# Hybrid layer on one core: the state-space layer's rotation tables for two groups and its other weights for four at once, on VectorE instead of GpSimd, and the states' product one group later

## The chip, the core and the metric

The kernel runs on one core of a Trainium2 chip. The time is that of one execution on the device, in microseconds (us). Five engines work side by side, each on a list of instructions in a fixed order: TensorE (PE, and PEld for its weight loads), VectorE (DVE), ScalarE (ACT), GpSimd (POOL), and SyncE (SP), which here only issues DMAs between DRAM and the core's memory, SBUF. PSUM is the memory that TensorE writes its products to. Times come from the hardware profiler's trace of one execution.

## What is computed

One decoder layer, depth 1, 2048 tokens of 1024 dimensions. After an RMS norm, one projection gives u, z_s, q, k, v and z_a of 512 columns each. u goes through a state-space layer, q, k and v through differential attention; both are gated, concatenated and projected back, and a second gated input is added. The change is in the state-space layer alone:

```python
ab_re = mag * jnp.cos(li * dt)
ab_im = mag * jnp.sin(li * dt)
...
bu_re = jnp.einsum('bsgp,gnp->bsgn', ug, bb_re)
bu_im = jnp.einsum('bsgp,gnp->bsgn', ug, bb_im)
...
_, _, xr, xi = lax.associative_scan(combine, (a_re, a_im, bu_re, bu_im), axis=1)
y = (jnp.einsum('bsgn,gpn->bsgp', xr, c_re.astype(f32))
     - jnp.einsum('bsgn,gpn->bsgp', xi, c_im.astype(f32)))
y = y.reshape(bsz, s_len, SSM_WIDTH) + d_skip.astype(f32) * uf
y = jax.nn.gelu(y)
y = y * jax.nn.sigmoid(y @ glu_w.astype(f32) + glu_b.astype(f32))
```

There are 32 groups (g) of 16 channels (p); each drives 64 complex states (n).

## The kernel before

**Phases.** Phase 1 (0 to some 745 us) makes the projections in 12 blocks of 512 columns, in the order u, u, then k, zs, v, q, za for the first half of the tokens and zs, k, v, q, za for the second. Every float32 factor is split into a pair of a rounded part (h) and a rest (l), and a product is three matmuls. The weights of a block come as eight tiles (`wraw`, line 275), are split by ScalarE (`wh`, 278) and VectorE (`wl`, 279), and lie in a ring of eight pairs, so that the next block's loads start as the last matmuls of this block let the ring go. Phase 2 is the attention, phase 3 the output.

**The state-space layer** runs in the background of phase 1: the generator `ssm` (309) is advanced a few steps after each quarter of a block. A scheduler that works from an estimate of durations and from priorities then fixes the order of each engine's list; background work has the lower priority.

**A group.** The tokens are cut into 256 chunks of 8 steps; a group's inputs U are 128 rows (8 steps by 16 channels) by 256 chunks. For each group the loop of line 563 does this:

- loads U (572), multiplies it with the norm's factors on GpSimd (573) and splits it (518, 519);
- makes the group's table of rotations `tab`, cosines and sines of 272 chunk phases: four products on GpSimd (584 to 587) and a difference and a sum on VectorE (588, 589);
- makes the weights out of the state, `wc`: three instructions on GpSimd (597 to 599) and a split;
- splits its part of the weights within a chunk, `mg`;
- multiplies `wa` with U into the first half of a PSUM bank (617), turns the result with the table (`rotate`, 604: three instructions `md`, `sw`, `md` on VectorE, two half copies `sw` on ScalarE), scans it over the chunks (`zz`, 621), turns it back and splits it (`xa`, 623);
- multiplies `mg` with U and then `wc` with `xa` into the second half of the bank (624, 625), and writes the result out (627, 628).

For each four groups, `four` (526) loads the parameters, makes `na` on GpSimd (534 to 538) and from it, on TensorE, `M` (through DRAM, 550 and 554) and `wa`. When all groups are done the GLU follows (line 676), for 256 tokens at a time.

Of the kernel before, what the change touches and what calls it, by code (L numbers as in the profile page):

```python
# [11 lines left out]
F32 = mybir.dt.float32  # L12
# [3 lines left out]
ALU = mybir.AluOpType  # L16
# [3 lines left out]
D = 1024  # L20
# [4 lines left out]
L = 8  # L25
# [34 lines left out]
TTB = 1  # L60
# [5 lines left out]
FA = 1  # L66
# [6 lines left out]
SSE = (1, 0, 0)  # L73
# [7 lines left out]
SPB = dict(U=2,wa=2,wc=2,mg=2,xa=1)  # L81
SPE = (1, 1, 1, 1)
# [5 lines left out]
SWB = 2  # L88
# [5 lines left out]
class Streamer:  # L94
    """Runs the making of a sequence of ring tiles ahead of their use."""
# [23 lines left out]
def hymba_kernel(ctx, tc, x_t, p_t, positions, norm_w, w_in, lam_re, lam_im, log_dt, b_re, b_im,  # L119
# [4 lines left out]
    TE, NE, UE = ((G, V)[v_] for v_ in SSE)  # L124
# [7 lines left out]
    NPAR = 9 * 2 + 16 * 4 + 16 * 2 + 17 * 2 + 1 + 9 * 2  # L132
    par_scr = [tc.dram_tile([128, 4, NPAR], F32, name=f"par_scr{i}") for i in range(8)]
    zs_scr = tc.dram_tile([512, S], F32, name="zs_scr")
# [19 lines left out]
    def reduce_angle(pool, src, shape, tag):  # L154
        """src - 2 pi round(src / 2 pi), and its cosine's angle; both within [-pi, pi]."""
# [8 lines left out]
        # a quotient next to a half may have been rounded away from its side  # L164
# [9 lines left out]
    def exp_exact(pool, out_, src, shape, tag):  # L174
        """exp to float32's accuracy: 2^k times a polynomial of the rest."""
# [17 lines left out]
    # ------------------------------------------------------------------ phase 1  # L193
    with ExitStack() as p1:
# [3 lines left out]
        # a place for each unit in the ring; what is used last lies lowest  # L198
# [13 lines left out]
        # -- x, split: units of 256 tokens, the model's dimensions on the partitions  # L212
# [32 lines left out]
        def squares(unit):  # L245
            """The mean squares of a unit's tokens, down the partitions."""
# [45 lines left out]
        # the first two units and the first weights, in the order of use  # L292
# [15 lines left out]
        # -- state-space layer, in the background of the projections  # L308
        def ssm():
            # tables of rotary embedding and small constants  # L310
            with tc.tile_pool(name="p1s", bufs=1) as sp:
# [16 lines left out]
                # lambda  # L328
# [12 lines left out]
                for nm, src in (("q", q_norm_w), ("k", k_norm_w)):  # L341
                    # the norm's weights: in the rotation's tables, and for what isn't turned down the partitions
# [846 lines left out]
```

## Time and profile before

| | us |
|---|---|
| median of three runs | 1517.39 |
| lowest and highest run | 1514.34, 1518.22 |
| span of the profiled execution (first to last instruction) | 1513.9 |
| TensorE busy in the span | 1423.3 (94%) |
| VectorE busy | 1015.2 (67%) |
| ScalarE busy | 755.2 (50%) |
| GpSimd busy | 648.0 (43%) |

The profiled execution's own time isn't listed apart from the three runs; its span is the part of it that the trace shows. "Busy" is the time in which an engine has an instruction running; matmuls are pipelined, one starting before the last has ended, so a busy TensorE isn't one at its peak. The shares are averages over phases with different limits; the rows further below are of the stage in which the change lies.

### The profile page before, as it was taken

Reading aid. Unit: us, or ns where it says so; the run is one execution under the profiler, and the core shown is the slowest. Engines: PE = TensorE matmul, PEld = TensorE weight load, DVE = VectorE, ACT = ScalarE, POOL = GpSimd, SP = SyncE. Lnnn points to the kernel's source line nnn. Section 1 sums busy time; section 2 is a strip of 40 time slices with the busy share of each in tenths; the row PEclk is TensorE's granted clock in tenths of the full one; section 3 lists DMA queues with packets and bytes.
Section 4 is the critical chain, followed back from the end, with each engine's and each line's share of the span. In section 5 each row is a group of like instructions: output and inputs, shape, how many; then the busy total and the mean of one; then the engine's idle time right before and its main releaser. Section 6 shows DMA issues by size and latency. Waiting matters only on the chain.

```text
span 1513.9 us, 27895 instructions
## 1 busy us (share of the span) xinstructions
PE 1423.3 (94%) x9794; PEld 1308.5 (86%) x9794; DVE 1015.2 (67%) x2489; ACT 755.2 (50%) x1711; POOL 648.0 (43%) x902
## 2 busy tenths in 40 slices
PE   7899988997988999999899999899999999999998
PEld 7898887776777888888789888898999999999998
DVE  8579899998999786665377767667779543222222
ACT  8443344544664455533358677677878541111111
POOL 5632666787757341132134445445434442221110
PEclk9999999999999999999999999999999999999999
DMA  7437824334553377634973543544426442111101
GB/s 237 137 114 249 278 82 138 126 88 143 178 155 103 118 187 201 167 119 152 241 213 97 153 137 108 156 122 122 136 80 208 126 152 91 64 63 64 63 22 43
DMA packets 208245, 205.56 MB, mean 136 GB/s; under 512 B 61016, under 2 KB 163560, under 8 KB 207080
## 3 DMA queue, kind: packets, MB, share of 16 engines
q1 hardware_dynamic: 208104, 203.78, 45.0%
q8 instruction: 77, 1.26, 0.3%
q14 instruction: 64, 0.52, 0.1%
HBM read 137.56 MB, written 74.55 MB: 140 GB/s over the span
## 4 chain that ended last, share of the span: by engine, by line
PE 52%; DVE 20%; DMA 12%; POOL 6%; issue 5%; ACT 3%; SPq 2%; DVEq 0%; ACTq 0%; POOLq 0%
PE pm L1125 11%; PE pss L1007 7%; PE pmf L892 7%; PE po L1043 7%; PE pmm L793 6%; PE pm L892 4%; PE ptw L1039 3%; PE pm L1129 3%; DMA wraw<-in_w_in_dram 3%; PE pss L676 2%; PE pmm L747 2%; DVE sw L611 2%; DVE md L612 1%; DVE wl L279 1%; DVE zz L621 1%
## 5 line engine op out<-in xcount | busy, mean ns | idle before, releaser
L793 PE MATMUL pmm<-wl,xh 128*128 128x512 f32 x512 | 202.9, 398 | 2.6 <-DVE wl L279 2.6
L793 PE MATMUL pmm<-wh,xh 128*128 128x512 f32 x512 | 200.2, 397 | 4.5 <-ACT wh L278 4.5
L793 PE MATMUL pmm<-wh,xl 128*128 128x512 f32 x512 | 202.4, 397 | 0.0
L1007 PE MATMUL pss<-ks,qd 128*128 128x512 f32 (+3 forms) x640 | 185.3, 388 | 5.5 <-DMA qd<-qh_scr 3.3
L1018 ACT ACTIVATE s<-s,st 128x1024 f32<-128x1024 f32 (+4 forms) x192 | 171.5, 896 | 35.7 <-DVE st L1009 32.6
L1043 PE MATMUL po<-vt,wt 128*128 128x128 f32 x1088 | 149.6, 276 | 2.3 <-ACT yo L1055 1.3
L1043 PEld LDWEIGHTS po<-vt,wt 128*128 128x128 f32 x1088 | 139.8, 191 | 10.0 <-ACT yo L1055 2.9
L1009 DVE CUSTOM_DVE_ANT_0 s<-pss,mk,st 128x512 f32<-128x512 f32 (+2 forms) x192 | 122.1, 650 | 39.3 <-PE pss L1007 37.9
L1125 PE MATMUL pm<-xh,wgh 128*128 128x256 f32 x512 | 141.3, 282 | 1.9 <-ACT xh L1095 1.8
L1125 PE MATMUL pm<-xh,wgl 128*128 128x256 f32 x512 | 142.8, 281 | 0.0
L1125 PE MATMUL pm<-xl,wgh 128*128 128x256 f32 x512 | 142.4, 281 | 0.0
L747 PE MATMUL pmm<-xh,wh 128*128 128x256 f32 x448 | 125.1, 293 | 8.9 <-DVE stg L757 4.0
L747 PE MATMUL pmm<-xh,wl 128*128 128x256 f32 x448 | 127.7, 289 | 0.7 <-DVE wl L279 0.7
L1133 DVE SCALAR_TENSOR_TENSOR th<-th,pm 128x256 f32<-128x256 f32 x64 | 26.7, 420 | 150.7 <-ACT th L1132 150.7
L747 PE MATMUL pmm<-xl,wh 128*128 128x256 f32 x448 | 127.1, 287 | 0.0
L1096 POOL TENSOR_TENSOR xl<-x,xh 128x512 fp32r<-128x512 f32 x32 | 43.2, 1366 | 179.7 <-PE pm L1125 110.7
L793 PEld LDWEIGHTS pmm<-wh,xh 128*128 128x128 f32 x512 | 97.9, 191 | 23.7 <-ACT wh L278 4.9
L793 PEld LDWEIGHTS pmm<-wl,xh 128*128 128x128 f32 x512 | 97.7, 191 | 23.3 <-DVE wl L279 5.0
L892 PE MATMUL pmf<-yh,woh 128*128 128x256 f32 x352 | 104.2, 296 | 11.5 <-ACT yh L882 9.0
L1007 PEld LDWEIGHTS pss<-ks,qd 128*128 128x128 f32 x640 | 101.3, 192 | 14.7 <-DVE st L1009 4.9
L793 PEld LDWEIGHTS pmm<-wh,xl 128*128 128x128 f32 x512 | 97.9, 191 | 18.3
L1132 ACT ACTIVATE th<-pm 128x256 f32<-128x256 f32 x64 | 24.3, 385 | 166.9 <-PE pm L1129 165.3
(360 smaller groups left out, 4294.5 us busy)
## 6 DMA issues: line engine op xcount, KB each, us to landing
wraw<-in_w_in_dram SPq DMA_DIRECT2D x96, 256.0 KB
xraw<-in_x_t_dram SPq DMA_DIRECT2D x40, 256.0 KB
qd<-qh_scr SPq DMA_DIRECT2D x64, 128.0 KB
qd<-ql_scr SPq DMA_DIRECT2D x64, 128.0 KB
xr<-in_x_t_dram SPq DMA_DIRECT2D x32, 256.0 KB
yin<-yt_scr SPq DMA_DIRECT2D x16, 512.0 KB
xp_scr<-xp SPq DMA_DIRECT2D x32, 256.0 KB
x<-xp_scr SPq DMA_DIRECT2D x8, 1024.0 KB
```

The source lines that it names most:

```text
L611: V.tensor_tensor(sw, sw, tabf[:, 1, first:first + NCH], op=ALU.mult)
L747: T.matmul(pm, lhsT=w[b_][:, cb * 128:cb * 128 + 128], rhs=xt[a_][:, k, :], start=(k == 0 and n == 0), stop=(k == 7 and n == 2))
L793: T.matmul(pm, lhsT=xt[a_][:, k, j * 128:j * 128 + 128], rhs=w[b_], start=(k == 0 and n == 0), stop=(k == 7 and n == 2))
L892: T.matmul(pm[:, e, :], lhsT=w[k][b_][:, ms], rhs=y[a_][:, k, :], start=(k == 0 and n == 0), stop=(k == 3 and n == 2))
L1007: T.matmul(pss[:, :cl], lhsT=qd[:, e, m, tq], rhs=ks[m][:, c0:c0 + cl], start=e == 0, stop=e == 1)
L1009: V.tensor_tensor_reduce(sr[m][pi][:, o:o + cl], pss[:, :cl], mk[:, end - cl:end], scale=1.0, scalar=3.4e38 if ci == 0 else st[:, 2 * ci - ...
L1018: A.activation(sr[m][pi][:, :cl], sr[m][pi][:, :cl], AF.Exp, bias=st[:, ci + m:ci + m + 1], scale=-1.0, accum_out=st[:, 12 + 2 * pi + m:13 ...
L1039: T.transpose(ptw[:, k, :], blocks_[kg + k], ident)
L1043: T.matmul(po[:, 0:128], lhsT=wt[:, k, :], rhs=vt[:, kg + k, :], start=kg + k == 0, stop=kg + k == len(blocks_) - 1)
L1096: G.tensor_tensor(xl, x1[:, n0:n0 + 2], xh.bitcast(F32), op=ALU.subtract)
L1125: T.matmul(pm[:, 0], lhsT=wg[0][k][b_][:, ms], rhs=xc[k // 2][a_][:, k % 2], start=(k == 0 and n == 0), stop=(k == 7 and n == 2))
L1129: T.matmul(pm[:, 1], lhsT=wp[0][k][b_][:, ms], rhs=pc_[a_][:, k], start=(k == 0 and n == 0), stop=(k == 1 and n == 2))
```

## The change

The setup makes the phase tables for half as many columns, with two groups over the 128 partitions (64 states each), and writes them to a DRAM array of their own (`ptab_scr`). `four` becomes a generator in four parts, advanced once a group: parameters and `na`; M and `wa`; the tables of the two pairs of groups; `wc` of all four groups. All of it but the mask of `dd` is on VectorE. A pair's table is written to DRAM (`tab_scr`) and read back in two halves for each group, so that both halves of the partitions hold it; the sign that was in the table is now in ScalarE's copy (`A.mul` with -1). The splits of `mg` and `wc` are made for four groups at once. U and the table of the next group are fetched one group ahead (`ahead`). All six products of U are issued together, and the product of the states is issued after the next group's (`behind`).

```diff
-SSE = (1, 0, 0)
+SSE = 0
...
-SPB = dict(U=2,wa=2,wc=2,mg=2,xa=1)
-SPE = (1, 1, 1, 1)
+SPB = dict(U=2, wa=2, wc=1, mg=1, xa=1)
...
-SWB = 2
+SWB = 1
...
-    TE, NE, UE = ((G, V)[v_] for v_ in SSE)
+    UE = (G, V)[SSE]
...
+                tp = sp.tile([128, NG // 2, NTAB], F32, name="tp")
...
+                def spread(par4, o_, l0):
+
+                    r_ = sp.tile(sh, F32, name="na", bufs=1)
+                    t_ = sp.tile([128, 2, 17, 16], F32, name="tabt", bufs=1).rearrange("q s a b -> q (s a b)")[:, :512]
+                    t_ = t_.rearrange("q (g l p) -> q g l p", g=4, l=L)
+                    V.tensor_tensor(r_, par4[:, :, o_:o_ + 16].unsqueeze(2).to_broadcast(sh),
+                                    par4[:, :, 65 + l0:73 + l0].unsqueeze(3).to_broadcast(sh), op=ALU.mult)
+                    V.tensor_tensor(t_, par4[:, :, o_ + 16:o_ + 32].unsqueeze(2).to_broadcast(sh),
+                                    par4[:, :, 74 + l0:82 + l0].unsqueeze(3).to_broadcast(sh), op=ALU.mult)
+                    V.tensor_tensor(r_, r_, t_, op=ALU.add)
+                    return r_
...
-                    G.tensor_tensor(na, par4[:, :, 18:34].unsqueeze(2).to_broadcast(sh),
-                                    par4[:, :, 150:158].unsqueeze(3).to_broadcast(sh), op=ALU.mult)
-                    G.tensor_tensor(nb, par4[:, :, 34:50].unsqueeze(2).to_broadcast(sh),
-                                    par4[:, :, 159:167].unsqueeze(3).to_broadcast(sh), op=ALU.mult)
-                    NE.tensor_tensor(na, na, nb, op=ALU.add)
...
+                    pt2 = sp.tile([128, 2, NTAB], F32, name="pt2", bufs=1)
+                    nc.sync.dma_start(pt2, ptab_scr[q4])
+                    na = spread(par4, 0, 1)
...
+                    for e in range(2):
+                        tx = sp.tile(sht, F32, name="tx", bufs=1)
+                        t1 = sp.tile(sht, F32, name="tabt", bufs=1)
+                        V.tensor_tensor(tx, pt2[:, e, 0:17].unsqueeze(1).unsqueeze(3).to_broadcast(sht),
+                                        pt2[:, e, 34:66].rearrange("q (s b) -> q s b", s=2).unsqueeze(2).to_broadcast(sht), op=ALU.mult)
+                        V.tensor_tensor(t1, pt2[:, e, 17:34].unsqueeze(1).unsqueeze(3).to_broadcast(sht),
+                                        pt2[:, e, 66:98].rearrange("q (s b) -> q s b", s=2).unsqueeze(2).to_broadcast(sht), op=ALU.mult)
+                        V.tensor_tensor(tx, tx, t1, op=ALU.add)
+                        nc.sync.dma_start(tab_scr[q4 * 2 + e], tx)
+                    yield
+                    wc = spread(par4, 32, 0)
+                    out_[q4] = par4, wa, M, wc
+                    yield
...
+                def ahead(g):
+
+                    U = sp.tile([128, NCH], F32, name="U", bufs=UB)
+                    nc.sync.dma_start(U, ug_scr[g].rearrange("l p c -> (l p) c"))
+                    UE.tensor_tensor(U, U, rl, op=ALU.mult)
+                    tab = sp.tile([128, 2, 17, 16], F32, name="tab")
+                    for d in range(2):
+                        nc.sync.dma_start(tab[d * 64:d * 64 + 64], tab_scr[g // 2][(g % 2) * 64:(g % 2) * 64 + 64])
+                    return split(U, "U", NCH), tab.rearrange("q s a b -> q s (a b)")
...
-                    G.tensor_tensor(tab[:, 0], ab[0], bb[0], op=ALU.mult)
-                    G.tensor_tensor(t1[:, 0], ab[1], bb[1], op=ALU.mult)
-                    G.tensor_tensor(tab[:, 1], ab[0], bb[1], op=ALU.mult)
-                    G.tensor_tensor(t1[:, 1], ab[1], bb[0], op=ALU.mult)
-                    TE.tensor_tensor(tab[:, 0], tab[:, 0], t1[:, 0], op=ALU.subtract)
-                    TE.tensor_tensor(tab[:, 1], tab[:, 1], t1[:, 1], op=ALU.add)
...
-                    wc = split(wc, "wc", 128, SPE[1])
...
-                    mg = split(M[:, :, gl * 16:gl * 16 + 16], "mg", 128, SPE[2])
...
+                    product(pst, [w_[:, gs] for w_ in wa4], U)
+                    product(py, [w_[:, gs] for w_ in mg4], U, last=False)
+                    if behind is not None:
+                        behind()
+                    if gl == 0:
+                        wc4 = split(wc_raw.rearrange("q g l p -> q (g l p)"), "wc", 512)
...
-                    product(pst, wa, U)
...
-                    product(py, mg, U, last=False)
-                    product(py, wc, xa, first=False)
...
+                    next(parts, None)
+                    if gl == 3 and g < NG - 1:
+                        mg4 = within(made[g // 4 + 1][2])
+                    if g < NG - 1:
+                        nxt = ahead(g + 1)
                     yield
+                behind()
```

What the scheduler makes of it is seen in the engines' lists. On TensorE, in the q block of the first half, before (`pss` is the bank of a group and `pmm` one of the projections; the number behind a name tells its instances apart):

```order
L524 MATMUL pss_3813<-Uh_3792,wah_3371 128x256
L524 MATMUL pss_3461<-xal_3487,wch_3457 128x256
L524 MATMUL pss_3461<-xah_3486,wcl_3458 128x256
L793 MATMUL pmm_4276<-wl_3608,xh_789 128x512
L524 MATMUL pss_3813<-Ul_3793,wah_3371 128x256
L524 MATMUL pss_3813<-Uh_3792,wal_3372 128x256
L524 MATMUL pss_3695<-Uh_3674,mgh_3696 128x256
L524 MATMUL pss_3695<-Ul_3675,mgh_3696 128x256
L524 MATMUL pss_3695<-Uh_3674,mgl_3697 128x256
```

and now, in the same block:

```order
L526 MATMUL pss_3612<-Uh_3436,wah_2784 128x256
L526 MATMUL pss_3612<-Ul_3437,wah_2784 128x256
L526 MATMUL pss_3612<-Uh_3436,wal_2785 128x256
L526 MATMUL pss_3612<-Uh_3436,mgh_3129 128x256
L526 MATMUL pss_3612<-Ul_3437,mgh_3129 128x256
L526 MATMUL pss_3612<-Uh_3436,mgl_3130 128x256
```

Before, a group's products with `wa` and with `mg` stood apart, with another group's between them (the `mg` products of 3813 begin 36 rows behind its first `wa` product); now the six products of one U stand in a row, and the products with `wc` follow apart from them.

On GpSimd, within the layer, before:

```order
L573 TENSOR_TENSOR U<-U,rl 128x256
L585 TENSOR_TENSOR tabt<-parg 128x272
L587 TENSOR_TENSOR tabt<-parg 128x272
L584 TENSOR_TENSOR tab<-parg 128x272
L586 TENSOR_TENSOR tab<-parg 128x272
L597 TENSOR_TENSOR wc<-parg 128x128
```

and now (`dd` is the skip's diagonal, `qst` the norm of queries and keys):

```order
L553 AFFINE_SELECT dd<-dd 128x64
L592 TENSOR_TENSOR U<-U,rl 128x256 x5
L553 AFFINE_SELECT dd<-dd 128x64
L592 TENSOR_TENSOR U<-U,rl 128x256 x2
L841 TENSOR_SCALAR qst<-qst 128x8
L842 TENSOR_TENSOR qst<-qst,negh 128x8
```

Of a group's eight instructions one, U's, has stayed there.

On SP, where the loads of the weights (`wraw`) follow the za block of the first half, before (`za_scr` takes that block's result, `yg_scr` a group's):

```order
L275 DMA wraw<-in_w_in_dram 128x512
L808 DMA za_scr<-t_5774 128x512
L628 DMA yg_scr<-ysb 128x256
L275 DMA wraw<-in_w_in_dram 128x512
L572 DMA U<-ug_scr 128x256
L275 DMA wraw<-in_w_in_dram 128x512 x3
```

and now, at the end of the same loads:

```order
L275 DMA wraw<-in_w_in_dram 128x512
L591 DMA U<-ug_scr 128x256
L275 DMA wraw<-in_w_in_dram 128x512
L595 DMA tab<-tab_scr_96 64x544 x2
L275 DMA wraw<-in_w_in_dram 128x512
L582 DMA tab_scr_97<-tx 128x544
```

The table's reads and the next table's write have come between the loads of the weights.

## Rows read from the trace of the kernel before

**Rows 1.** One stretch: busy us per engine (instructions), clock, DMA share, GB/s.

```profile
190.00:500.00 310.00, 271.84 (x1556) 233.26 (x1554) 292.20 (x576) 156.49 (x380) 219.84 (x287) 0.96 0.41 125
```

**Rows 2.** VectorE's groups, 190 to 500 us: busy us, mean ns, idle us.

```profile
L612 DVE TENSOR_TENSOR md<-md,sw 128x256 f32<-128x256 f32 x60 | 37.1, 618 | 0.5
L611 DVE TENSOR_TENSOR sw<-sw,tab 128x256 f32<-128x256 f32 x60 | 34.0, 568 | 4.2 <-ACT sw L610 3.6
L279 DVE SCALAR_TENSOR_TENSOR wl<-wraw,nw,wh 128x512 fp32r<-128x512 f32 x32 | 27.4, 864 | 5.6 <-ACT wh L278 5.6
L621 DVE TENSOR_TENSOR_SCAN zz<-parg,md 128x256 f32<-128x256 f32 x30 | 25.4, 848 | 0.3
L519 DVE TENSOR_TENSOR Ul<-U,Uh 128x256 fp32r<-128x256 f32 x31 | 21.3, 687 | 0.0
L519 DVE TENSOR_TENSOR xal<-md,xah 128x256 fp32r<-128x256 f32 x29 | 19.2, 663 | 0.0
L588 DVE TENSOR_TENSOR tab<-tab,tabt 128x272 f32<-128x272 f32 x30 | 18.9, 630 | 2.2 <-POOL tab L584 1.7 <-POOL tabt L585 0.5
L608 DVE TENSOR_TENSOR md<-zz,tab 128x256 f32<-128x256 f32 x30 | 16.8, 559 | 0.5
L519 DVE TENSOR_TENSOR mgl<-M,mgh 128x128 fp32r<-128x128 f32 x32 | 16.0, 500 | 0.0
L589 DVE TENSOR_TENSOR tab<-tab,tabt 128x272 f32<-128x272 f32 x30 | 15.9, 529 | 0.0
L519 DVE TENSOR_TENSOR wcl<-wc,wch 128x128 fp32r<-128x128 f32 x29 | 13.3, 460 | 1.9 <-ACT wch L518 1.8
```

**Rows 3.** VectorE, whole span: shortest, median, longest ns by line.

```profile
L612 DVE TENSOR_TENSOR md<-md,sw x64: 408/456/1296, 192.7 to 515.2; 128x256 f32<-128x256 f32 x64
...
L608 DVE TENSOR_TENSOR md<-pss,tab x32: 405/412/426, 189.2 to 506.0; 128x256 f32<-128x256 f32 x32
...
L621 DVE TENSOR_TENSOR_SCAN zz<-parg,md x32: 675/694/1771, 194.4 to 512.2; 128x256 f32<-128x256 f32 x32
...
L279 DVE SCALAR_TENSOR_TENSOR wl<-wraw,nw,wh x96: 721/750/1775, 5.4 to 702.5; 128x512 fp32r<-128x512 f32 x96
...
L519 DVE TENSOR_TENSOR wal<-pss,wah x8: 675/678/679, 187.4 to 460.7; 128x512 fp32r<-128x512 f32 x8
```

**Rows 4.** TensorE's waits, 190 to 500 us: total us, times, longest us.

```profile
PE pss L524 <- DVE xal L519: 11.3, 14, 1.9
PE pmm L793 <- ACT wh L278: 4.5, 1, 4.5
PE pss L524 <- ACT sw L610: 3.2, 5, 1.1
```

**Rows 5.** GpSimd's groups, 190 to 500 us, of the kinds that stay.

```profile
L573 POOL TENSOR_TENSOR U<-U,rl 128x256 f32<-128x256 f32 x31 | 29.4, 949 | 26.3 <-DVE zz L620 12.3 <-DMA U<-ug_scr 5.9 <-DVE t L772 2.8
...
L815 POOL TENSOR_TENSOR qst<-qst,negh 128x8 f32<-128x8 f32 x8 | 14.4, 1797 | 0.4
...
L546 POOL TENSOR_SCALAR_AFFINE_SELECT dd<-dd 128x64 f32<-128x64 f32 x6 | 2.7, 444 | 10.2 <-DMA dd<-in_ssm_d_dram 10.2
```

**Rows 6.** Timeline at 336 us: start us, duration us, engine.

```profile
335.84 1.72 POOL L815 TENSOR_TENSOR qst<-qst,negh 128x8 f32<-128x8 f32 x1
...
336.10 0.41 DVE L519 TENSOR_TENSOR Ul<-U,Uh 128x256 fp32r<-128x256 f32 x1
```

**Rows 7.** Two stretches of projections alone: as rows 1.

```profile
50.00:60.00 10.00, 10.00 (x86) 10.00 (x85) 6.88 (x22) 3.61 (x7) 5.98 (x10) 1.00 0.45 117
680.00:690.00 10.00, 10.00 (x48) 8.29 (x47) 4.92 (x13) 1.27 (x2) 4.37 (x6) 1.00 0.32 105
```

**Rows 8.** Timeline of the first group: U's multiplication and the first product.

```profile
178.97 0.74 POOL L573 TENSOR_TENSOR U<-U,rl 128x256 f32<-128x256 f32 x1
...
187.46 0.28 PE L524 MATMUL pss<-Uh,wah 128*128 128x256 f32 x1
```

**Rows 9.** ScalarE's waits, 190 to 500 us: total us, times, longest us.

```profile
ACT wh L278 <- DMA wraw<-in_w_in_dram: 16.8, 11, 7.3
```

More of the change, by code (lines that the diff above doesn't have):

```diff
@@ L59 @@
 XRB = 3
-TTB = 1
 GLE = (0, 2)
@@ L65 @@
 BGS = (1, 0)
-FA = 1
 KOUT = (0, 3)
@@ L536, in four @@
-                    G.tensor_tensor(nb, par4[:, :, 34:50].unsqueeze(2).to_broadcast(sh),
-                                    par4[:, :, 159:167].unsqueeze(3).to_broadcast(sh), op=ALU.mult)
-                    NE.tensor_tensor(na, na, nb, op=ALU.add)
-                    pr_ = ps_ss.tile([128, 512], F32, name="pss")
-                    for g in range(4):
-                        T.matmul(pr_[:, g * 16:g * 16 + 16], lhsT=na[:, g].rearrange("q l p -> q (l p)"),
-                                 rhs=par4[:, g, 50:66], start=True, stop=True)
+                    pt2 = sp.tile([128, 2, NTAB], F32, name="pt2", bufs=1)
@@ L547, in four @@
                                     fill=0.0, base=-112, channel_multiplier=1)
+                    yield
+                    pr_ = ps_ss.tile([128, 512], F32, name="pss")
+                    for g in range(4):
+                        T.matmul(pr_[:, g * 16:g * 16 + 16], lhsT=na[:, g].rearrange("q l p -> q (l p)"),
+                                 rhs=par4[:, g, 32:48], start=True, stop=True)
                     rs = sp.tile([128, 64], F32, name="rs", bufs=1)
@@ L557, in four, with within @@
                         T.transpose(pw_[:, g * 128:g * 128 + 128], na[:, g].rearrange("q l p -> q (l p)"), ident)
-                    wa = split(pw_, "wa", 512, 1)
-                    return par4, wa, M
-                nxt = four(0)
+                    wa = split(pw_, "wa", 512)
+                    yield
+                    sht = [128, 2, 17, 16]
+                    for e in range(2):
[7 more added lines that the diff above has]
+                        nc.sync.dma_start(tab_scr[q4 * 2 + e], tx)
+                    yield
+                    wc = spread(par4, 32, 0)
+                    out_[q4] = par4, wa, M, wc
+                    yield
+                def ahead(g):
[3 more added lines that the diff above has]
+                    tab = sp.tile([128, 2, 17, 16], F32, name="tab")
+                    for d in range(2):
+                        nc.sync.dma_start(tab[d * 64:d * 64 + 64], tab_scr[g // 2][(g % 2) * 64:(g % 2) * 64 + 64])
+                    return split(U, "U", NCH), tab.rearrange("q s a b -> q s (a b)")
+                def within(M):
+                    return split(M.rearrange("q l (g p) -> q g l p", g=4), "mg", 512)
+                made = {}
+                for _ in four(0, made):
+                    pass
+                mg4 = within(made[0][2])
+                nxt = ahead(0)
+                behind = None
                 yield
@@ L564, in ssm @@
                     gl = g % 4
+                    gs = slice(gl * 128, gl * 128 + 128)
                     if gl == 0:
[L566 to L572 removed]
@@ L598, in ssm @@
-                    G.tensor_tensor(nb, q1b, K2.unsqueeze(1).to_broadcast(shl), op=ALU.mult)
-                    NE.tensor_tensor(wc, wc, nb, op=ALU.add)
-                    wc = split(wc, "wc", 128, SPE[1])
-                    bank = ps_ss.tile([128, 512], F32, name="pss")
-                    mg = split(M[:, :, gl * 16:gl * 16 + 16], "mg", 128, SPE[2])
+                        par4, wa4, _, wc_raw = made.pop(g // 4)
+                        parts = four(g // 4 + 1, made) if g < NG - 4 else iter(())
```

110 lines of the change are left out of this document (44 added, 66 removed).

## The prediction

> **What bounds the kernel now.** I read the table of stretches first, since the average over the span hides the stage that is changed. From 190 to 500 us, while 30 of the 32 groups of the state-space layer run behind the projections, VectorE is busy 292.2 of 310 us (94%) and TensorE 271.8 [rows 1]. So TensorE has 38 us idle there, and its granted clock is 0.96 on average, which is 12 us more of lost work. It isn't the bound. VectorE is.
>
> Next, what VectorE does there, line by line [rows 2]. The 256-element instructions of one rotation (md, sw) cost 618, 568 and 559 ns on average, and the same shapes have run in 408 ns; the same multiplication with its source in PSUM (md<-pss) never took more than 426 ns in all 32 runs [rows 3]. So a third of what these lines cost is waiting of some kind, and it strikes instructions whose two inputs both lie in SBUF. GpSimd is busy 219.8 us of the same 310 [rows 1], nearly all with two-input work on SBUF.
>
> Last, who TensorE waits for [rows 4]: xal 11.3 us and sw 3.2 us, both the states' rotation on VectorE and ScalarE, and once 4.5 us for weights.
>
> **The change part by part.** The sum is made for the stage from 190 to 500 us of the profiled execution, whose span is 1513.9 us; the median of the three runs, 1517.4, lies 3.5 us above that span, and the sum's difference is put to the median.
>
> *Removed from VectorE.* The two closing instructions of each group's table (18.9 + 15.9 us), and the splits of the within-chunk weights (mgl, 16.0) and of the weights out of the state (wcl, 13.3): 64.1 us [rows 2].
>
> *Added to VectorE.* Per two groups, three instructions of 544 elements for the table; per four groups, six of 512 (the two spreads) and two splits of 512. A 512-element two-input instruction has 678 ns (wal, [rows 3]) and a 256-element one 408, so 1.05 ns an element, and 544 elements come to 0.71 us. For 30 groups that is 15 x 3 x 0.71 = 32.0 and 7.5 x 8 x 0.678 = 40.7, together 72.7 us. wal has one source in PSUM and the new ones broadcast both sources from SBUF; no row shows that on VectorE. If they paid what md<-md,sw pays over its floor (618 against 408 ns, [rows 2, 3]), they would cost half as much again, 109 us. Below 72.7 they can't go, since that is the price of the same element count undisturbed. I take 72.7: the disturbing instructions are the ones that leave. Net +8.6 us, at worst +45.
>
> *Relief.* What stays on VectorE (md, sw, zz, Ul, xal and the weights' wl) costs more than its floor by 60 x 0.210 + 60 x 0.160 + 30 x 0.173 + 31 x 0.279 + 29 x 0.255 + 30 x 0.151 + 32 x 0.143 = 52 us [rows 2, 3], with 408 ns as the floor of all 256-element ones. On GpSimd five kinds stay, from U (29.4 us) to dd (2.7), with three qst lines between: 54.3 us [rows 5]. So 165.5 of 219.8 us leave. But the long qst instruction doesn't disturb: while one ran from 335.84 for 1.72 us, Ul took its 0.41 us [rows 6]. Counting U alone as what goes on disturbing, 165.5 / (165.5 + 29.4) = 85% of the 52 us goes, 44 us. Bounds: 0, if the excess is something else, and 52.
>
> The Trainium skill (SBUF — State Buffer, section "Who interferes with whom") says that a VectorE instruction with two SBUF inputs contends with a GpSimd instruction that reads SBUF, and that the loser blocks for the whole instruction. By the forms that are slow here and the PSUM form that isn't, the trace agrees; in the row at 335.84 us it doesn't, since a GpSimd instruction that reads SBUF ran and nothing was held. By the rule qst would keep on disturbing, 75% would go instead of 85%, 39 us, and the time below would be some 5 us longer.
>
> *Sum on VectorE.* 292.2 + 8.6 - 44 = 256.8 us. If VectorE is then busy as large a part of the stage as now, 256.8 / 0.943 = 272 us instead of 310: -38, and for 32 groups instead of 30, -40.
>
> *The states' product one group later.* Now a group's product within the chunk waits until both halves of the rotation have read the bank, and its last product follows a few matmuls behind xal. In the new order all six products of U stand together, and xal has a group's time. That takes away the 11.3 and 3.2 us of waits [rows 4]. It is no second gain: these waits are where TensorE feels VectorE's lateness, and they lie within the 38 us.
>
> *The start.* The first product stands 92 matmuls of the zs block earlier than before; a 10 us stretch holds 86 of them [rows 7], so 10.7 us earlier. Before, it ran at 187.46 us [rows 8]. Its operands come no 10 us earlier: U was multiplied at 178.97 for 0.74 us [rows 8], with a cast and Ul (0.41 each) behind it, so 180.6 us at the earliest, while TensorE is there at 176.8. I charge the difference, 4 us, with 0 and 10.7 as the bounds (M now has to be back from DRAM at once too).
>
> *DMAs.* Tables go out once per two groups and come back in two halves per group: 16 + 64 more transfers on SP's queue, 8 + 8 for their parameters. The transfers are covered by the group's time that they have; what stands behind them in the queue is the first rival of the other sign, below. The table of half as many groups in the setup shortens VectorE's work ahead of 160 us, where TensorE doesn't wait for it: 0.
>
> *The end.* The last product of the layer stands 137 matmuls later, and the GLU behind it too. After GLU's last matmul 306 of the 512-element matmuls of the projections still follow before and 169 in the new order; at 48 matmuls in 10 us [rows 7] that is 35 us of cover left: 0.
>
> Total: -40 + 4 = -36 us, 1517.4 - 36 = 1481.
>
> **The rivals.** *TensorE becomes the bound.* If the relief is complete and the decoupling takes the rest, all 38 us idle and the 12 us of clock go: 1517 - 50 + 4 = 1471, and less if the short gaps that pipelined matmuls hide in "busy" go too. For it: at full relief VectorE would need 249 us for work in which TensorE is busy 272 [rows 1]. Against it: weights and DMA make waits of their own (4.5 us for wh).
>
> *The relief doesn't come.* The excess may be the price of broadcast and small tiles rather than of GpSimd. Then VectorE has 300 us or more to do, and only the waits on xal and sw go: -14.5, with 4 to 10.7 us lost at the start: 1507 to 1514. For it: the new instructions have forms that no row prices. Against it: md<-pss with its steady 412 ns.
>
> *SP's queue takes VectorE's place: slower.* The table's write waits for VectorE, its reads wait for the buffer that the rotation two groups back still reads, and in the new order they stand among the loads of the next block's weights. At a block's change eight such loads are due at once; ScalarE already waits 16.8 us for them, 7.3 at the longest [rows 9], and TensorE's single 4.5 us is that wait. The stage has six such changes. From 36 / 6 = 6 us each the gain is gone; at 8.5 us each the kernel is at 1532. Against it: SP already waits for Ul with U's load in just that place, and these waits shrink with VectorE's work.
>
> That the change doesn't do what it says is excluded by the order of GpSimd's instructions, where tables and weights are gone.
>
> **How the numbers follow.** Forecast 0.45 (1476 to 1490), TensorE as the bound 0.22, no relief 0.20, SP's queue 0.13. The predicted time is the forecast's, 1481. About 0.3% (4.6 us) is what a measurement of this kernel can tell from no change, so "same" is 1512.8 to 1522: of the no-relief case 0.06 falls there, and 0.02 of the SP case. Faster: 0.45 + 0.22 + 0.14 = 0.81; same 0.08; slower 0.11. For 8 in 10 the range needs the forecast, the TensorE case with its hidden gaps and most of the no-relief case: 1456 to 1513.
>
> **What would show it.** In the new profile, over the stretch of the layer: md, sw and xal near 410 ns; the table's instructions at 0.71 us; VectorE's busy time down by some 35 us; TensorE's waits on xal and sw gone; the first product of the layer behind a wait of some 4 us. I am wrong if md<-zz stays above 500 ns with GpSimd idle, if the 544-element instructions cost 1 us, or if ScalarE's wait for wraw grows to tens of us.

## The result, and the profile after

Four runs of the changed kernel took 1476.78 to 1481.17 us, median 1479.18; four of the kernel before 1512.88 to 1518.22, median 1515.87. The ratio is 0.9754, with a 95% interval of 0.9732 to 0.9776: 36.7 us less. The prediction was 1481, from 1456 to 1513. The profiled execution took 1478.0 us with a span of 1476.3.

Where the time went is seen when the span is cut at the last 512-element matmul of the projections, the end of phase 1. That matmul starts at 740.9 us in the kernel before and at 704.6 now; from there to the end it is 773.0 us before and 771.7 now. So 36.3 of the 37.6 us are gone ahead of that point.

The stretch from 190 to 500 us, columns as in [rows 1]:

```profile
190.00:500.00 310.00, 299.94 (x1791) 261.87 (x1791) 273.83 (x609) 167.10 (x361) 62.11 (x70) 0.99 0.58 177
```

TensorE is busy 28.1 us longer in the same 310 us and does 235 more matmuls; its idle time is 10.1 us instead of 38.2. GpSimd is down from 219.8 to 62.1 us. VectorE is down from 292.2 to 273.8, although it does the work of 31 groups instead of 30 and of more projections. The layer itself isn't shorter: its first product starts at 187.5 us and its last at 519.4 before, at 175.0 and 511.4 now. The projections get on faster beside it.

VectorE's groups by line in this stretch (line, operation, out<-in, count, busy us, mean ns, idle before):

```profile
L279 DVE SCALAR_TENSOR_TENSOR wl<-wraw,nw,wh 128x512 fp32r<-128x512 f32 x40 | 29.9, 751 | 6.6 <-ACT wh L278 6.5
L633 DVE TENSOR_TENSOR md<-md,sw 128x256 f32<-128x256 f32 x61 | 27.3, 448 | 0.7
L632 DVE TENSOR_TENSOR sw<-sw,tab 128x256 f32<-128x256 f32 x62 | 27.1, 437 | 4.8 <-ACT sw L631 4.5
L640 DVE TENSOR_TENSOR_SCAN zz<-parg,md 128x256 f32<-128x256 f32 x31 | 21.8, 703 | 0.4
L521 DVE TENSOR_TENSOR xal<-md,xah 128x256 fp32r<-128x256 f32 x30 | 13.6, 455 | 1.6 <-ACT xah L520 1.4
L629 DVE TENSOR_TENSOR md<-zz,tab 128x256 f32<-128x256 f32 x31 | 13.3, 430 | 0.4
L629 DVE TENSOR_TENSOR md<-pss,tab 128x256 f32<-128x256 f32 x31 | 12.9, 415 | 0.0
L521 DVE TENSOR_TENSOR Ul<-U,Uh 128x256 fp32r<-128x256 f32 x30 | 12.5, 415 | 3.2 <-ACT Uh L520 3.2
L537 DVE TENSOR_TENSOR tabt<-parg 128x512 f32<-128x512 f32 x15 | 11.0, 731 | 0.8 <-DMA parg<-par_scr 0.7
L539 DVE TENSOR_TENSOR na<-na,tabt 128x512 f32<-128x512 f32 x15 | 10.7, 715 | 0.0
L577 DVE TENSOR_TENSOR tx<-pt 128x544 f32<-128x544 f32 x14 | 10.6, 756 | 13.4 <-DMA tab_scr<-tx 13.4
L579 DVE TENSOR_TENSOR tabt<-pt 128x544 f32<-128x544 f32 x14 | 10.0, 712 | 0.0
L581 DVE TENSOR_TENSOR tx<-tx,tabt 128x544 f32<-128x544 f32 x14 | 9.9, 711 | 0.0
L535 DVE TENSOR_TENSOR na<-parg 128x512 f32<-128x512 f32 x14 | 9.5, 680 | 0.0
...
L521 DVE TENSOR_TENSOR wcl<-na,wch 128x512 fp32r<-128x512 f32 x8 | 6.4, 806 | 0.2 <-ACT wch L520 0.2
...
L521 DVE TENSOR_TENSOR mgl<-M,mgh 128x512 fp32r<-128x512 f32 x7 | 4.8, 686 | 0.0
```

md, sw, xal and Ul come from 559 to 687 ns [rows 2] down to 415 to 455; md<-pss, with one input in PSUM, stays at 415 as it was at 412. TensorE's waits in the stretch (total us, times, longest us):

```profile
PE pmm L820 <- ACT wh L278: 2.3, 2, 1.3
...
PE pss L526 <- DVE xal L521: 0.5, 1, 0.5
```

The 11.3 us on xal and the 3.2 on sw [rows 4] have become 0.5 and nothing.

### The profile page after: what moved, and what is told of

The parts are those of the page before. It is cut to its first block, busy times and chain, and to the rows that moved or that the text cites. A ratio compares the mean times of both kernels' runs of the same rounds, so it can differ in the third digit from the quotient of the medians.

```text
span 1476.3 us, 27658 instructions
## 1 busy us (share of the span) xinstructions
PE 1409.7 (95%) x9794; PEld 1299.4 (88%) x9794; DVE 971.7 (66%) x2477; ACT 749.0 (51%) x1663; POOL 468.8 (32%) x654
## 4 chain that ended last, share of the span: by engine, by line
PE 40%; DMA 7%; ACT 2%; DVE 2%; POOL 1%; issue 1%; SPq 1%; DVEq 0%; ACTq 0%; POOLq 0%
PE pm L1152 11%; PE po L1070 6%; PE pss L1034 6%; PE pmf L919 6%; PE pm L919 4%; PE pm L1156 3%; PE ptw L1066 3%; DMA yin<-yt_scr 2%; DMA ks<-kh_scr 1%; DMA yin<-in_ple_w_gate_dram 1%; DMA qd<-ql_scr 1%; DMA yt_scr<-yo 1%; ACT s L1045 1%; DMA xr<-in_x_t_dram 0%; SPq L990 0%
## 5 line engine op out<-in xcount | busy, mean ns | idle before, releaser
L820 PE MATMUL pmm<-wh,xh 128*128 128x512 f32 x512 | 197.1, 395 | 3.7 <-ACT wh L278 2.3
L1070 PEld LDWEIGHTS po<-vt,wt 128*128 128x128 f32 x1088 | 139.6, 191 | 10.6 <-ACT yo L1082 3.2
L919 PE MATMUL pmf<-yl,woh 128*128 128x256 f32 x352 | 101.6, 289 | 2.0 <-POOL yl L910 2.0
```

The costliest lines, as they stand in the source:

```text
L820: T.matmul(pm, lhsT=xt[a_][:, k, j * 128:j * 128 + 128], rhs=w[b_], start=(k == 0 and n == 0), stop=(k == 7 and n == 2))
L919: T.matmul(pm[:, e, :], lhsT=w[k][b_][:, ms], rhs=y[a_][:, k, :], start=(k == 0 and n == 0), stop=(k == 3 and n == 2))
L1070: T.matmul(po[:, 0:128], lhsT=wt[:, k, :], rhs=vt[:, kg + k, :], start=kg + k == 0, stop=kg + k == len(blocks_) - 1)
```

## The experiments

*Excess* in the table is VectorE's time over its floors from 190 to 500 us: for md (but not md<-pss), sw, zz, Ul, xal and wl, the count times the mean less the floor of [rows 3]; 52.5 us before, 8.6 now. *Phase 1* is the start of the last 512-element matmul of the projections, and *rest* what the span has behind that. The ratio is to the kernel before in the same session.

| kernel | ratio (95%) | median us | excess | PE, DVE, POOL busy, 190 to 500 | phase 1 | rest |
|---|---|---|---|---|---|---|
| before | 1 | 1512.6 to 1515.9 | 52.5 | 271.8, 292.2, 219.8 | 740.9 | 773.0 |
| changed | 0.9754 (0.9732 to 0.9776) | 1479.2 | 8.6 | 299.9, 273.8, 62.1 | 704.6 | 771.7 |
| e1_own_group | 0.9730 (0.9705 to 0.9754) | 1472.6 | 8.0 | 297.9, 270.8, 65.3 | 701.0 | 765.8 |
| e2_tables_gpsimd | 1.0041 (1.0021 to 1.0061) | 1518.3 | 52.9 | 274.6, 265.7, 158.0 | 741.2 | 775.1 |
| e3_gp_two_inputs | 1.0036 (1.0019 to 1.0053) | 1517.7 | 40.8 | 275.4, 286.8, 172.9 | 749.8 | 769.1 |
| e4_gp_one_input | 0.9903 (0.9880 to 0.9925) | 1498.9 | 22.1 | 287.9, 281.5, 237.0 | 725.7 | 771.2 |
| e6_dve_more | 0.9847 (0.9813 to 0.9880) | 1489.7 | 10.0 | 293.3, 274.6, 64.0 | 714.8 | 775.7 |
| e7_u_on_vector | 0.9835 (0.9801 to 0.9869) | 1488.6 | 3.6 | 294.4, 265.4, 33.3 | 712.6 | 775.4 |
| e8_before_on_vector | 0.9817 (0.9783 to 0.9852) | 1486.1 | 7.4 | 302.5, 290.4, 78.5 | 706.7 | 779.0 |
| e9_own_group_u_on_vector | 0.9820 (0.9776 to 0.9865) | 1486.4 | 3.7 | 300.2, 271.3, 38.6 | 702.7 | 780.9 |
| e10_before_more_room | 1.0044 (1.0025 to 1.0064) | 1520.7 | 40.0 | 290.3, 262.3, 188.3 | 740.6 | 776.2 |
| e11_own_group_more_room | 0.9822 (0.9792 to 0.9852) | 1488.0 | 7.6 | 302.4, 260.7, 70.8 | 704.2 | 782.4 |
| e12_tables_gpsimd_more_room | 0.9992 (0.9974 to 1.0010) | 1513.3 | 51.5 | 287.7, 250.9, 145.2 | 731.4 | 783.1 |
| e13_two_tx | 0.9832 (0.9806 to 0.9858) | 1490.4 | 9.4 | 297.2, 273.9, 64.8 | 710.9 | 777.8 |

Every edit makes the scheduler lay out new lists, so that two kernels differ by more than their edit says. Eight kernels have a small excess and end phase 1 between 701.0 and 714.8 us, however they are built: these 14 us, and 15 in the rest (765.8 to 780.9 us where the GLU doesn't end late, see e10 below), are taken as what lists can differ by. They hold the edits' own effects too (e6 adds work, and has the 714.8), so they are an upper bound; no difference of that size between two kernels is put down to an edit below.

### The product one group later, undone (e1_own_group)

```diff
+                    behind()
+                    behind = None
                     next(parts, None)
...
                     yield
-                behind()
```

> The changed kernel with one part undone: the product of the states (wc with xa) is issued in its own group again, behind that group's own rotation. Everything else is as in the changed kernel. Theory (the gain is VectorE's shorter work, and the waits on xal were only where TensorE felt it late): md and xal stay near their floors (450 and 456 ns on average now), the waits on xal and sw stay under 5 us, and the time is within 5 us of 1479. Rival (the later product is a gain of its own): the waits on xal and sw come back with 14 us or more, and the time is 1490 or above.

It took 1472.6 us, with excess and phase 1 as in the changed kernel. TensorE's wait on xal from 160 to 700 us:

```profile
PE pss L526 <- DVE xal L521: 0.4, 1, 0.4
```

So the rival falls: the waits on xal went with the contention, and the later product isn't a gain of its own. The time is 1.4 us beyond the 5 that the theory allowed, on the faster side; with the two ratios' intervals overlapping, that is no difference that these runs show.

### The engine alone undone (e2_tables_gpsimd)

```diff
-                    V.tensor_tensor(r_, par4[:, :, o_:o_ + 16].unsqueeze(2).to_broadcast(sh),
+                    G.tensor_tensor(r_, par4[:, :, o_:o_ + 16].unsqueeze(2).to_broadcast(sh),
...
-                        V.tensor_tensor(tx, tx, t1, op=ALU.add)
+                        G.tensor_tensor(tx, tx, t1, op=ALU.add)
```

(so for all three instructions of `spread` and all three of a table)

> The changed kernel with its six instructions for every two groups (three of 544 elements for a table, three of 512 of a spread) back on GpSimd, batched as they are. Theory (GpSimd's two-input work holds VectorE's): GpSimd gets some 120 us more to do in the layer's stage, against 165 us that the change took away, so md, sw and xal rise to some 530 to 590 ns on average; that gives VectorE back 33 us, while 64 us leave it, so its busy time in the stage falls to some 243 us and the time stays at 1475 to 1482, since TensorE is the bound by now. Rival (GpSimd's slowness itself, its part in the chain, was the cost, and not what it does to VectorE): md stays near 450 ns and the time goes to 1495 or above.

1518.3 us: the whole gain is lost. Two of VectorE's groups by line, 190 to 500 us:

```profile
L632 DVE TENSOR_TENSOR sw<-sw,tab 128x256 f32<-128x256 f32 x62 | 39.6, 640 | 6.6 <-ACT sw L631 6.2
L633 DVE TENSOR_TENSOR md<-md,sw 128x256 f32<-128x256 f32 x62 | 36.6, 590 | 1.1
```

and the stretch:

```profile
190.00:500.00 310.00, 274.60 (x1575) 237.20 (x1574) 265.68 (x488) 154.28 (x340) 157.95 (x142) 0.95 0.54 168
```

The contention came as the theory said, 590 and 640 ns, and the rival's 450 didn't. But the time that the theory made of it, 1475 to 1482, is off by 36 us; the rival's 1495 or above did come. VectorE is busy 265.7 us of 310 here, less than in the changed kernel, and yet TensorE idles 35.4. VectorE's sum doesn't set the stage. TensorE's two longest waits, 160 to 700 us, are on what VectorE makes late: xah is ScalarE's copy of the rotation's result, and waits for md on VectorE.

```profile
PE pss L526 <- ACT xah L520: 9.9, 7, 3.5
PE pss L526 <- DVE mgl L521: 5.5, 5, 3.0
```

That GpSimd's own slowness in the chain costs the time, the other half of the rival, is for the next two runs to tell: their added work has nobody waiting for it but the next U.

### GpSimd loaded again, by itself (e3_gp_two_inputs, e4_gp_one_input)

```diff
                     UE.tensor_tensor(U, U, rl, op=ALU.mult)
+                    for _ in range(6):
+                        G.tensor_tensor(rl, rl, ones[:, 0:1].to_broadcast([128, NCH]), op=ALU.mult)
```

> The changed kernel with six more GpSimd instructions a group that nothing waits for but the next U: the norm's factors times a one, in place, 128x256, two inputs in SBUF. Theory (contention): some 150 us more of GpSimd in the stage, about what the change took away; md, sw and xal back at 560 to 660 ns, VectorE's busy time up by some 40 us, and the time at 1500 to 1520, that of the kernel before. Rival (the excess over 408 ns came from the forms, the tables' making or its dependencies): md, sw and xal stay under 470 ns and the time is within 5 us of 1479.

and with `G.tensor_scalar(rl, rl, 1.0, None, op0=ALU.mult)` in its place:

> As the run with two-input instructions on GpSimd, but with six of one input in SBUF: the norm's factors times the constant 1, in place, 128x256. By the Trainium skill (SBUF — State Buffer, section "Who interferes with whom") any GpSimd instruction that reads SBUF does it: then md, sw and xal rise per us of GpSimd's busy time as they do with two inputs. Theory after the row at 335.84 us (a qst instruction that held nothing): one input holds less, md stays under 480 ns and the time within 5 us of 1479.

GpSimd's added group and VectorE's md and sw, 190 to 500 us, with two inputs:

```profile
L594 POOL TENSOR_TENSOR rl<-rl,ones 128x256 f32<-128x256 f32 x159 | 125.8, 791 | 11.6
```

```profile
L635 DVE TENSOR_TENSOR md<-md,sw 128x256 f32<-128x256 f32 x52 | 30.8, 593 | 0.6
...
L634 DVE TENSOR_TENSOR sw<-sw,tab 128x256 f32<-128x256 f32 x52 | 28.5, 548 | 1.6 <-ACT sw L633 1.4
```

and with one:

```profile
L594 POOL TENSOR_SCALAR rl<-rl 128x256 f32<-128x256 f32 x179 | 184.2, 1029 | 13.7
```

```profile
L635 DVE TENSOR_TENSOR md<-md,sw 128x256 f32<-128x256 f32 x60 | 30.0, 500 | 0.7
L634 DVE TENSOR_TENSOR sw<-sw,tab 128x256 f32<-128x256 f32 x59 | 28.0, 474 | 3.4 <-ACT sw L633 3.0
```

Work on GpSimd whose result is the number that was there already takes the ratio from 0.9754 to 1.0036, all of the gain, as the theory said (VectorE's busy time in the window grew by 13 and not by 40 us, since fewer groups fall into it: 52 md<-md instead of 61). With one input the ratio is 0.9903, between the two expectations: 179 such instructions add 13.5 us of excess (22.1 - 8.6), 0.08 us each, and 159 of the others 32.2, 0.20 us each. So GpSimd's busy time isn't the measure, 237.0 us being the most of all kernels, and U's wait behind a busier GpSimd isn't the cost either; which instructions run there counts. Rows of the timelines say the same: a 256-element md, sw, Ul or xal of VectorE with only the two-input one beside it ran 0.33 us longer than its shortest time (mean of 71 rows, 0.45 at most), with only the one-input one 0.08 (132 rows, 0.23 at most). By the Trainium skill (SBUF — State Buffer, section "Who interferes with whom") an instruction of GpSimd that reads SBUF contends with a two-input one of VectorE, and the rule makes no difference by the number of its inputs. These runs do: one input held, but less than half as much, though each such instruction ran longer (1029 ns against 791).

### The engine alone changed (e8_before_on_vector)

```diff
-                    G.tensor_tensor(tab[:, 0], ab[0], bb[0], op=ALU.mult)
+                    V.tensor_tensor(tab[:, 0], ab[0], bb[0], op=ALU.mult)
...
-                    G.tensor_tensor(wc, p1b, K1.unsqueeze(1).to_broadcast(shl), op=ALU.mult)
+                    V.tensor_tensor(wc, p1b, K1.unsqueeze(1).to_broadcast(shl), op=ALU.mult)
```

(so for the four products, for all three instructions of `wc` and for all three of `na`)

> The kernel before with only the engine changed: a group's seven instructions for its table and its weights out of the state, and the three of the spread for four groups, on VectorE instead of GpSimd; nothing batched, nothing later. VectorE gets 30 x (4 x 0.43 + 3 x 0.27) + 7 x 3 x 0.68 = 90 us more and loses some 44 us of contention: 338 us for a stage of 310. Theory: VectorE is then over its limit and the time is 1530 to 1550; the batching for two and four groups is what makes the move pay. Rival (leaving GpSimd is the gain, whatever it costs on VectorE): 1500 or less.

It took 1486.1 us, 27.6 below the median of the kernel before in its session, where the theory said 1530 to 1550; the rival's 1500 or less is what came. The stretch:

```profile
190.00:500.00 310.00, 302.47 (x1788) 266.97 (x1787) 290.44 (x793) 163.50 (x379) 78.45 (x74) 0.99 0.44 137
```

VectorE is as busy as before (290.4 against 292.2 us) and TensorE idles 7.5 us instead of 38.2. This is the clearest row of the study: with the tables off GpSimd, a VectorE at 94% holds TensorE up hardly at all. VectorE's added work makes the layer in the background last longer (27 scans in the stretch instead of 30, the last product at 549.4 us), and the projections go on beside it. Phase 1 ends at 706.7 us, close to the changed kernel's 704.6, so the engine alone brings that gain. In the changed kernel the layer ends earlier, at 511.4 us. The later product isn't the reason, since e1_own_group ends it at 511.4 too; batching and fetching ahead are left, and no run parts them. Whether they add time can't be told, since the 9 us between the two kernels by their ratios are within what lists differ by.

### VectorE loaded, and relieved (e6_dve_more, e7_u_on_vector, e9_own_group_u_on_vector)

After e2 a second theory stood beside the first: not VectorE's sum costs, but single late instructions against lists that were planned without contention.

```diff
-                    V.tensor_tensor(l_, x_, h_.bitcast(F32), op=ALU.subtract)
+                    for _ in range(3 if nm == "U" else 1):
+                        V.tensor_tensor(l_, x_, h_.bitcast(F32), op=ALU.subtract)
```

> The changed kernel with the split of U's rest on VectorE done three times instead of once for each group (the same result each time): two more undisturbed 256-element instructions a group, 25 us more of VectorE in the layer's stage, GpSimd as in the changed kernel. Theory one (VectorE's sum sets the stage, as the prediction had it): VectorE's busy time in the stage goes from 274 to some 295 of 310 us and the time to 1495 to 1505. Theory two (TensorE is the bound by now and VectorE's lists have slack; what costs is that contention makes single instructions of the rotation late against the order that was planned): the time stays within 8 us of 1479, and TensorE's waits in the stage grow by less than 8 us.

1489.7 us lies between the two. VectorE's busy time in the stretch hardly rose (274.6 us, not 295), since the layer ends 35 us later and fewer groups fall into it; TensorE's idle time there grew by 6.6 us. Phase 1 is 10.2 us longer and the rest 4.0. It is no proof for either.

```diff
-SSE = 0
+SSE = 1
```

(on the changed kernel in e7, on e1_own_group in e9)

> The changed kernel with U's multiplication on VectorE too, so that GpSimd keeps only the mask of dd and the qst lines. VectorE gets 31 x 0.41 = 13 us more and, if U was what still disturbed it, loses the 8.6 us by which md, sw, zz, xal and wl still lie over their shortest times. If contention with two-input GpSimd instructions is the cause: md and sw at 408 to 420 ns. If qst disturbs too (12 of 1.8 us in the stage): md and sw stay at some 430 ns. Time within 5 us of 1479 if TensorE is the bound; 1485 or more if VectorE's sum is.

> The changed kernel with the states' product in its own group again and with U's multiplication on VectorE: the two variants that might each take a little off, together. If the later product costs some 3 to 7 us, as the run with it undone made it look, and U's move is neutral: 1468 to 1476. If that run's lead was the luck of its order: 1479 again.

md and sw came to 420 ns both and the excess to 3.6 us (3.7 in e9), with eleven long qst lines of 1.7 us still there in e7: U was what still disturbed, and qst doesn't. The times, 1488.6 and 1486.4, are 9 and 14 us above the kernels with U on GpSimd. They fit no expectation but the 1485 or more that was given to VectorE's sum, and VectorE is busy 8.4 us less in the stretch in e7 than in the changed kernel. In e7 TensorE idles 15.7 us there, without one wait that stands out; in e9 phase 1 ends at 702.7 and the loss lies in the rest. Why it is lost isn't settled, and no more is lost than lists differ by.

### More room between groups (e10, e11, e12)

```diff
-BGP = [2, 1, 2] * 3 + [1, 2, 1] * 5 + [4] * 18
+BGP = [1, 1, 1] * 8 + [2] * 4 + [4] * 14
```

(e10 on the kernel before, e12 on e2_tables_gpsimd, e11 on e1_own_group)

> The kernel before with only the pace of the layer changed: one step of the layer for each quarter of a block where it had one or two, so that 1578 of the projections' 512-element matmuls stand between its first and last product instead of 1276 (1505 in the changed kernel, 1621 in the one with the tables on VectorE unbatched). The work of each engine is the same, GpSimd's too. Theory two (the lists were planned for undisturbed durations and too close; what contention adds comes out as TensorE's waits): with more projections between two groups VectorE's lateness is covered, the waits on xal and sw go, and the time falls to 1485 to 1500 while md, sw and xal stay at 550 to 660 ns. Rival (contention and the table work on VectorE cost time whatever the spacing): within 6 us of the kernel before.

> The changed kernel with its batched tables and spreads on GpSimd, at the slower pace: 1658 projection matmuls between the first and last product instead of 1321. Contention is as in that kernel at the faster pace (md and sw near 600 ns). If it was the close spacing that let the contention through to the time: 1475 to 1490 instead of 1518. If the contention costs by itself: 1505 or more.

> The changed kernel with the states' product in its own group and the same slower pace: 1686 projection matmuls between the layer's first and last product instead of 1498, with 32 left behind the GLU's last matmul instead of 195. If TensorE still waits for the layer because it is planned too close, the 12 us that it idles in the stage shrink and the time is 1464 to 1471. If TensorE is the bound with what is left, the time stays at 1470 to 1476, and it rises to 1480 or more if 32 matmuls are too few to cover the GLU's end.

The second theory falls with the first of them: 1520.7 us, 4.9 above the kernel before, with phase 1 at the same 740.6. TensorE's waits from 160 to 700 us:

```profile
PE pss L524 <- DVE xal L519: 10.6, 11, 2.9
...
PE pss L524 <- ACT sw L610: 4.0, 5, 1.0
```

10.6 and 4.0 us stand where 11.3 and 3.2 stood [rows 4], though the groups stand further apart. From 190 to 500 us TensorE idles less than before (19.7 us instead of 38.2), but the layer now goes on to 574.5 us, and from 160 us to the end of phase 1 it idles 47.7 us where it idled 46.0. Room between groups doesn't cover what is late within one. With GpSimd's load batched, e12, phase 1 gains 9.8 us, the rest loses 8.0, and the 1505 or more of the other expectation stands. In e11, where contention was gone already, phase 1 is 3 us longer and the rest 16.6. The expectation had 32 matmuls as too few behind the GLU for that case. In e8, e10, e11 and e12 the GLU's last matmul stands 7 to 10 us ahead of the projections' last, and the rest is 776 to 783 us, the upper half of all; in the changed kernel it is 39 us ahead, with 771.7. But e9 has 780.9 with 30 us and e13 below 777.8 with 61, so the late GLU isn't shown to be the reason.

### The new wait on VectorE (e13_two_tx)

In the changed kernel VectorE waits for the table before, which is written to DRAM from the same buffer (190 to 500 us):

```profile
DVE tx L577 <- DMA tab_scr<-tx: 13.4, 6, 4.9
```

```diff
-                    r_ = sp.tile(sh, F32, name="na", bufs=1)
+                    r_ = sp.tile([128, 2, 17, 16], F32, name="tx", bufs=2).rearrange("q s a b -> q (s a b)")[:, :512]
+                    r_ = r_.rearrange("q (g l p) -> q g l p", g=4, l=L)
...
-                        tx = sp.tile(sht, F32, name="tx", bufs=1)
+                        tx = sp.tile(sht, F32, name="tx", bufs=2)
```

(on e1_own_group; `dd` has one buffer instead of two, for the space)

> The kernel with the states' product in its own group (1472.6), and the new wait of the change taken away: VectorE idles 13 to 15 us in all before the first multiplication of a table, until the table made before it has been written to DRAM from the same buffer. Here tables and spreads share a ring of two buffers. If that idle time reaches TensorE: the wait falls to under 3 us and the time to 1462 to 1469. If VectorE's idle time there is covered: the wait falls and the time stays at 1470 to 1476. Slower than that would mean that the new order of the lists costs more than the wait did.

The wait fell from 14.6 us to 8.1, not to under 3, and the time rose to 1490.4, which fits only the last sentence of the expectation: phase 1 is 9.9 us and the rest 12.0 us longer than in e1_own_group. The wait's own price stays open; phase 1 of e1_own_group, with the wait in it, is the shortest of all. e1_own_group and the changed kernel are thus the fastest that ran.

## Why the prediction was right, and where its working wasn't

**The added work** was 72.7 us for 30 groups; the eight new groups of lines in the stretch after sum to 11.0 + 10.7 + 10.6 + 10.0 + 9.9 + 9.5 + 6.4 + 4.8 = 72.9 (for 101 instructions, where the working counted 105). Broadcast from SBUF on both sides costs nothing that shows: 680 ns on average for 512 elements (line 535), where wal had 678 [rows 3].

**The relief** was 44 of 52 us; the excess went from 52.5 to 8.6, by 43.9. VectorE's whole busy time from 160 us to the end of phase 1 fell from 467.7 to 425.9 us, by 41.8, where the working had 35 for 30 groups. Row by row the cause is plain. In the timeline of the kernel before, 190 to 500 us, md (but not md<-pss), sw, Ul and xal stand in 208 rows of their own. In 81 of them GpSimd ran no two-input instruction but qst's within the first 0.408 us: these took 0.007 us more than 0.408 on average, 0.042 at most. The other 127 took 0.33 more, up to 1.08. In the changed kernel the 29 beside a multiplication of U took 0.17 more, and the 30 beside qst or dd 0.009, no more than the 155 with nothing beside them (0.008). So the rest was U's and none of it qst's.

How U does it stands in single pairs of rows. The timeline of the changed kernel (start us, duration us, engine):

```profile
166.43 0.72 POOL L592 TENSOR_TENSOR U<-U,rl 128x256 f32<-128x256 f32 x1
166.55 1.19 DVE L577 TENSOR_TENSOR tx<-pt 128x544 f32<-128x544 f32 x1
```

```profile
175.31 0.88 POOL L592 TENSOR_TENSOR U<-U,rl 128x256 f32<-128x256 f32 x1 [0.86 <-DMA U<-ug_scr]
...
175.50 1.23 DVE L535 TENSOR_TENSOR na<-parg 128x512 f32<-128x512 f32 x1
```

Line 577 has run in 698 ns and line 535 in 674. Begun 0.12 and 0.19 us behind a multiplication of U, they took 0.49 and 0.56 us longer, somewhat less than what U's had still to go. By the Trainium skill (SBUF — State Buffer, section "SBUF: two separate sides") whichever of the two starts first has the shared ports for its whole instruction, and the other blocks. With two inputs on both sides these rows agree, within 0.13 us.

**From VectorE's sum to the time** is the step that failed. The prediction took VectorE as the bound, since it was 94% busy, and had the stage shrink with its sum, 256.8 / 0.943. But e2 has less on VectorE in the stretch than the changed kernel and the time of before; e8 has as much as before and nearly the time of the changed kernel. From 160 us to the end of phase 1 VectorE is busy 435.2 us in e2 (75%) and 461.7 in e8 (84%): the one with less is the slower by 34.5 us at that point. What sorts the kernels is the excess: 40 to 53 us of it with phase 1 at 731 to 750, 22 us with 726, 10 us or less with 701 to 715. Within the first of these three it orders nothing (e3 with 40.8 is the latest), as 24 to 31 groups fall into the stretch. The forecast's number is thus in part luck: the sum fell by the same relief, and by about what that was worth to TensorE, and no run shows that it had to.

**TensorE as the bound**, the rival with 0.22, describes the stage after better than the forecast: TensorE busy 97% of it, VectorE 88%. Its price was 38 us of idle time and 12 of clock; 28.1 of the idle went, and the mean granted clock rose from 0.96 to 0.99, some 9 us of 310. That is 37, where the rival had 50: 10 us of idle are left, no one cause of which comes to more than 2.3 us. How idle time and the clock stand together is seen in the kernel before:

```profile
300.00:310.00 10.00, 6.81 (x35) 5.34 (x33) 10.00 (x13) 5.26 (x12) 9.41 (x10) 0.97 0.49 142
310.00:320.00 10.00, 9.84 (x35) 7.26 (x36) 10.00 (x19) 5.02 (x13) 8.18 (x12) 0.68 0.57 177
```

TensorE has 3.2 us of 10 idle, and in the next 10 us the granted clock is 0.68 on average (between the two levels of 1.2 and 2.4 GHz), with 35 matmuls done where the 10 us after that have 50, at 1.00. Not every gap is followed by such a fall: from 450 to 460 us TensorE was busy the same 6.81 us, and the clock was 1.00 there and in the next 10 us. Among the 31 stretches of 10 us from 190 to 500 us six were granted under 0.95 before (310 to 320 among them) and one now, 380 to 390, with 0.83.

**The later product** was said to be no second gain; e1 confirms it.

**The start** was charged 4 us, for operands that come late. They came early: U was multiplied at 166.4 us, and the first product ran at 175.0, without a wait. The 180.6 us of the working were read off GpSimd's list of before, where U stands behind eight instructions that left with the change:

```profile
173.47 1.08 POOL L534 TENSOR_TENSOR na<-parg 128x512 f32<-128x512 f32 x1 [2.07 <-DMA dd<-in_ssm_d_dram]
...
175.56 0.65 POOL L584 TENSOR_TENSOR tab<-parg 128x272 f32<-128x272 f32 x1
...
177.74 0.65 POOL L584 TENSOR_TENSOR tab<-parg 128x272 f32<-128x272 f32 x1
```

(three of those between 173.47 us and U at 178.97, [rows 8]). The stretch from 160 to 190 us still lost about 3 us: 1.5 more of idle, and a granted clock of 0.89 instead of 0.94. TensorE's waits there are 3.2 us for a wl of the projections and 1.6 for mgh. The size was right, for another reason.

**The queue of SP** didn't come: ScalarE's waits for wraw are 17.4 us where they were 16.8 [rows 9], with 40 tiles loaded in the stretch instead of 32, and the longest is 3.5 instead of 7.3, and TensorE waits for wh 2.3 us in two waits (0.3 more in the z_s block) where it waited 4.5 in one [rows 4].

```profile
ACT wh L278 <- DMA wraw<-in_w_in_dram: 17.4, 13, 3.5
```

**The end** was charged nothing: the rest is 771.7 us against 773.0, and the GLU's last matmul stands 39 us ahead of the projections' last, where the working had 35 of cover.

**That no relief comes** is refuted by the excess; **the wait on tab_scr**, 13.4 us on VectorE, was named nowhere.

## What to carry to other kernels

A high busy share of VectorE beside a busy GpSimd isn't yet a bound: compare the mean with the shortest time of each shape, and with the same operation reading PSUM. Here the two differed by a third, and with GpSimd's two-input work away TensorE's waits went, even where VectorE then had as much to do as before. The work that moved lengthens what runs in the background; with batching and fetching ahead that ended at 511 instead of 549 us here. And if work is taken out of a queue, read the times of what stays in it anew.

## What the runs showed that wasn't expected

- ScalarE isn't touched by the contention: wh has 720 ns and xah 404 and 405 in the kernels before and after alike.
- The cost of contention to TensorE isn't VectorE's lost time in sum. Why 44 us of excess on an engine that isn't full (265.7 of 310 us in e2) cost TensorE some 25 us of idle isn't settled. Single long instructions are a candidate (md<-md up to 1296 ns [rows 3]); wider spacing of the groups, e10, wasn't the cure, and no run held the lists fixed.
- Lists that the scheduler lays out for similar work give phase 1 ends up to 14 us apart. How much of that is the lists' and how much the edits' no run parts, so that single edits of this kernel can't be judged below some 1%.
